# Expert products of 64 stationary columns in place of two of 32, in a mixture-of-experts encoder block

## The chip, the cores and the metric

The kernel runs on one core of a Trainium2 chip. The metric is the device time of one execution in microseconds, as the median of three runs. A profile comes from one further execution, which has a time of its own.

## The reference, cut to what matters

The block is one layer: a mixer (a gated DeltaNet and a short convolution, side by side), then a mixture of experts, each behind a modulated RMSNorm with a gated residual, and a last RMSNorm. There are 256 positions of width 1024, and all data are float32. The change touches only the experts:

```python
logits = hf @ router_w + router_b            # 256 tokens, 32 experts
top_val, top_idx = lax.top_k(logits, 4)      # each token goes to 4 experts
gates = softmax(top_val)
...
gu = x_blk @ w1[e] + b1[e]                   # w1[e]: 1024 x 2048
gate, up = split(gu, 2)
act = min(gate, 7) * sigmoid(1.702 * gate) * (clip(up, -7, 7) + 1)
yb = act @ w2[e] + b2[e]                     # w2[e]: 1024 x 1024
...
y = segment_sum(yb * gate_of_token)          # back to the 256 tokens
```

## The kernel before

**Stages.** The mixer and the routing come first. The experts begin at about 427 us of the profiled execution, and it is their stage that the change touches. The weights of all 32 experts (w1 8 MB and w2 4 MB each) are read once from HBM, in float32, through a ring of buffers (`wst`) that SP's queue fills in program order.

**Slots.** Experts are taken four at a time, in eight quads `q`. A quad has 256 slots, in eight groups of 32. `GROUPS` (line 31) says how many groups each of the four experts has: (2, 2, 2, 2) in the first quad, (3, 1, 2, 2) in the other seven. A quad is two pairs `p = 2*q + pa`, each with two experts `m` and four groups of slots, 128 slots in all. So the owners of the four groups of a pair are 0, 0, 1, 1 in both pairs of quad 0 and in the second pair of every quad, and 0, 0, 0, 1 in the first pair of quads 1 to 7 (p = 2, 4, ..., 14).

**Products.** The tokens of the slots are the stationary operand and the weights are the moving one. `w1_pair` (line 1409) goes over eight blocks `k` of 128 rows of w1 and four stretches `c` of 512 columns of it; for each (k, c) it issues four products of 32 stationary columns, one for each group of slots, at `tile_position=(0, 32 * j)`. Each of them writes its own 32 partitions of the accumulator `pss[c]`. `Second.block` (line 1459) does the same with the activations `aT` and w2, for eight blocks `f` and two halves `h`, in place of four stretches. `w2_cols` (line 1479) does it for the last pair, in three parts of the columns. Below, the four products of one (k, c) or (f, h) are called a set. All these products are issued by the helper `mm` (line 1336), so they all carry line 1337 in the profile; they are told apart by their operands: `acc<-wst,XT` for w1 and `acc<-wst,aT` for w2.

**Order.** The order of TensorE's work is that of the program (`held = [pin]`). In the loop over pairs (line 1674) the first product of pair p comes first, then the second product of pair p - 1 by blocks, and between the blocks hang the small steps: transposes of the activations (`to_ff`), the gather of the next quad's tokens (`gather_part`), and the combine step (`combine`), whose products are 128 columns wide. Each pair begins with four bias products (`w1_bias`, line 120), so the rows of line 120 mark the pairs in time.

**Two other places** are used below for comparison. `three_pass` (lines 312 to 314) issues the mixer's projections, most of them with 128 stationary columns; its call from `ba_mm` (line 447) has 32 and no tile position. Lines 943 and 944 issue two products of 64 stationary columns at `tile_position=(0, 64 * h)`.

Of the kernel before, what the change touches and what calls it, by code (L numbers as in the profile page):

```python
# [21 lines left out]
KT = D // 128  # L22
# [8 lines left out]
GROUPS = ((2, 2, 2, 2), (3, 1, 2, 2))  # L31
# [22 lines left out]
def encoder_block(ctx, tc, x, c, ada_w, ada_b, norm1_w, w_in, conv_qkv_w, a_log, dt_bias, onorm_w,  # L54
# [59 lines left out]
    def acc():  # L114
        return pm.tile([128, 512], FT, name="acc", tag=next(accs), bufs=3)

    def w1_bias(pa, bsel, b1c, pss, parts=(0, 1, 2, 3), first=False, pinned=False):
        for c in parts:
            b = 32 * c
            i = PE.matmul(pss[c], bsel[b:b + 32, pa * 128:(pa + 1) * 128], b1c[b:b + 32], start=first, stop=not first,  # L120
                          tile_position=(b, 0), skip_group_check=True)
            if pinned:
                tc.keep_in_program_order(i)
# [10 lines left out]
    with ExitStack() as mix:  # L134
# [119 lines left out]
        class Job:  # L254
            def __init__(self, load, cut, mm, post=None, lo="v"):
                self.load, self.cut, self.mm, self.post, self.lo, self.parts = load, cut, mm, post, lo, None
# [95 lines left out]
        for j in range(4):  # L352
# [12 lines left out]
            w = ep.tile([128, KT, 256], FT, name="raw", tag="raw", bufs=6) \  # L365
# [13 lines left out]
            for kk in range(2):  # L379
                k = 2 * j + kk  # L380
# [118 lines left out]
        for d in range(2):  # L499
            m = masks[:, d]  # L500
# [488 lines left out]
        def load_rows(srcs, hold=lambda i: i):  # L989
            _, halves = slot()  # L990
            for h, src in zip(halves, srcs):
                hold(nc.sync.dma_start(h, src))
            return halves
# [14 lines left out]
        def w1_load(p, k, regs):  # L1008
            if p < 2 or p == 2 * NQ - 1 and k >= KT - 2:
                return pre.pop((p, k), None) or w1_rows(p, k, regs)  # L1010
            if k % 2 == 0:
                c = 256 * (k // 2)
                held_w[0] = [load_unit(w1_src(p, m, regs)[:, c:c + 256]) for m in range(2)]
            return [quarters(h[k % 2]) for h in held_w[0]]
# [157 lines left out]
        def flat(x):  # L1172
            for it in x:
                if isinstance(it, (list, tuple)):
                    yield from flat(it)
                else:
                    yield it
        tail, n = list(flat(late_items)), 0
# [143 lines left out]
    for p, k, m, ts in ((0, KT - 1, 0, [spare("g"), spare("g"), spare("u"), spare("th")]),  # L1322
                        (0, KT - 1, 1, [spare("ysb"), spare("ysb"), spare("pg"), spare("pgT")]),
                        (1, 4, 0, [spare("aT", 1024), spare("aT", 1024)]), (1, 4, 1, [e4, fw])):
        o, qs = 0, []
        c = 256 * (k // 2) + k % 2
        for t in ts:
            n = t.shape[1]
# [7 lines left out]
    def mm(*a, **kw):  # L1336
        return held[0](PE.matmul(*a, **kw))  # L1337
# [17 lines left out]
    def gather_part(P, xq, ks):  # L1355
        p = misc()
        for kk, k in enumerate(ks):
            o = p[:, kk * QS:(kk + 1) * QS]
            n = 0
            for t in range(2):  # L1360
                for hx in (h2h, h2l):
                    mm(o, hx[:, t, 256 * (k // 2) + k % 2:256 * (k // 2) + k % 2 + 255:2], P[:, t],
                                  start=n == 0, stop=n == 3, skip_group_check=True)
                    n += 1
        for kk, k in enumerate(ks):
            o = p[:, kk * QS:(kk + 1) * QS]
            if k % 2:
                V.tensor_scalar(xq[:, k], o, facp[:, k:k + 1], facp[:, 8 + k:9 + k], op0=OP.mult, op1=OP.add)  # L1368
            else:
                A.activation(xq[:, k], o, AF.Identity, scale=facp[:, k:k + 1], bias=facp[:, 8 + k:9 + k])  # L1370
# [15 lines left out]
        A.copy(gt, p.rearrange("p (a t n) -> p a t n", a=2, t=2))  # L1386
        return gt

    def owners(q):
        return [m for m, g in enumerate(GROUPS[min(q, 1)]) for _ in range(g)]  # L1390

    def swiglu(n, g_ps, u_ps):
        g = work.tile([128, 512], FT, name="g", tag="g", bufs=2)
# [14 lines left out]

    def w1_pair(p, xq, bsel, pss, regs, mids):
        q, pa = divmod(p, 2)  # L1410
        own = owners(q)[4 * pa:4 * pa + 4]
        if p:
            w1_bias(pa, bsel, b1c, pss, first=True, pinned=True)
        for k in range(KT):
            w = w1_load(p, k, regs)
            for c in (0, 2, 1, 3):
                for j in range(4):
                    mm(pss[c][j * 32:(j + 1) * 32], xq[:, k, (4 * pa + j) * 32:(4 * pa + j + 1) * 32],
                                  w[own[j] % 2][c], start=False, stop=k == KT - 1,
                                  tile_position=(0, 32 * j), skip_group_check=True)  # L1420
            if p == 0 and k < KT - 2:
                gather_part(P0, xq, (k + 2,))
            for f in mids.get(k, ()):
                f()
        return [swiglu(128, pss[half], pss[2 + half]) for half in range(2)]
# [18 lines left out]
    def w2_rows(p, m, regs):  # L1444
        return moe_w2[0, 2 * p + m:2 * p + m + 1] if p < 2 else moe_w2[0, ds(regs[2 * (p % 2) + m], 1)]
# [7 lines left out]
    class Second:  # L1453
        def __init__(self, p, aT, gt, regs):
            self.p, self.aT, self.gt, self.regs = p, aT, gt[:, p % 2], regs
            self.own = owners(p // 2)[4 * (p % 2):4 * (p % 2) + 4]
            self.ys = [acc() for _ in range(2)]

        def block(self, c):
            if self.p < 2 or self.p == 2 * NQ - 2:  # L1460
                w = load_rows([w2_rows(self.p, m, self.regs)[:, 512 * (c // 2):512 * (c // 2) + 512]
                               .rearrange("e (p s r) n -> s p (e r n)", s=2, r=2)[c % 2] for m in range(2)])
            else:
                if c % 2 == 0:
                    self.w = [load_unit(w2_rows(self.p, m, self.regs)[:, 256 * c:256 * c + 512]) for m in range(2)]
                w = [h[c % 2] for h in self.w]
            w = [h.rearrange("p (i n) -> p i n", i=2) for h in w]
            for i in range(2):
                f = 2 * c + i
                for h in range(2):  # L1470
                    for j in range(4):
                        mm(self.ys[h][j * 32:(j + 1) * 32], self.aT[:, f, j * 32:(j + 1) * 32],
                           w[self.own[j] % 2][:, i, 512 * h:512 * h + 512], start=f == 0, stop=f == KT - 1,
                           tile_position=(0, 32 * j), skip_group_check=True)

        def end(self):
            return [lambda h=h, y=scaled(self.ys[h], 512 * h, 512): combine([self.gt], [y], 512 * h, 512) for h in range(2)]

    def w2_cols(p, parts, aT, gt, regs):
        q, pa = divmod(p, 2)  # L1480
        own = owners(q)[4 * pa:4 * pa + 4]
        c0, n = parts[0][0], sum(n for _, n in parts)
        ys = [acc() for _ in parts]
        nc_ = 2 if n > 256 else 4
        for c1 in range(0, 4, nc_):
            w = []
            for m in range(2):
                src = w2_rows(p, m, regs)[:, 256 * c1:256 * c1 + 256 * nc_, c0:c0 + n]
                if n > 256:
                    w.append(load_unit(src, 2 * n, True))  # L1490
                else:
                    _, halves = slot()
                    for h in range(2):
                        nc.sync.dma_start(halves[h][:, 0:4 * n].rearrange("p (i n) -> p i n", n=n),
                                          src[:, 512 * h:512 * h + 512].rearrange("e (p i) n -> p (e i) n", i=4))
                    w.append([halves[c // 2][:, 2 * n * (c % 2):2 * n * (c % 2) + 2 * n] for c in range(4)])
            w = [[h[:, 0:2 * n].rearrange("p (i n) -> p i n", i=2) for h in hs] for hs in w]
            for c in range(nc_):
                for i in range(2):
                    f = 2 * (c1 + c) + i  # L1500
                    for y, (o, no) in zip(ys, parts):
                        for j in range(4):
                            mm(y[j * 32:(j + 1) * 32, 0:no], aT[:, f, j * 32:(j + 1) * 32],
                                          w[own[j] % 2][c][:, i, o - c0:o - c0 + no], start=f == 0, stop=f == KT - 1,
                                          tile_position=(0, 32 * j), skip_group_check=True)
        return [lambda o=o, no=no, y=scaled(y, o, no): combine([gt[:, pa]], [y], o, no) for y, (o, no) in zip(ys, parts)]

    gtf_box = []
# [100 lines left out]
    xq = xq_tile()  # L1609
# [64 lines left out]
    for p in range(NP):  # L1674
        q, pa = divmod(p, 2)
# [32 lines left out]
        if 0 < p < NP - 1:  # L1708
# [4 lines left out]
            if pa and q + 1 < NQ:  # L1713
                xq = xq_tile()
# [28 lines left out]
    with tc.If(n_over > 0):  # L1743
        ov = work.tile([128, KT, 128], FT, name="over", tag="aT", bufs=2).rearrange("p b n -> p (b n)")
        V.tensor_tensor(rks[:, 0], rks[:, 0], capr[:, None, :].to_broadcast([128, 2, NE]), op=OP.subtract)
        with tc.For_i(0, NE, 1) as cp:
# [6 lines left out]
            with tc.For_i(0, nb, 1) as b:  # L1753
# [7 lines left out]
                p = misc()  # L1761
                for k in range(KT):
                    n = 0
# [8 lines left out]
                p = misc()  # L1772
# [4 lines left out]
                for half in range(2):  # L1777
                    pss = [acc() for _ in range(2)]
                    for gu in range(2):
                        bs = slice(32 * (2 * gu + half), 32 * (2 * gu + half) + 32)  # L1780
                        PE.matmul(pss[gu][0:32], ohe[bs].to_broadcast([NE, 32]), b1c[bs],
                                  start=True, stop=False, tile_position=(bs.start, 0), skip_group_check=True)
                    for k in range(KT):
                        wo = wp_box[0].tile([128, 2, 512], FT, name="wst", tag="u5")
                        for gu in range(2):
                            c0 = gu * FF + half * 512
                            nc.sync.dma_start(wo[:, gu], moe_w1[0, ds(e, 1), k * 128:(k + 1) * 128, c0:c0 + 512]
                                              .rearrange("e p n -> p (e n)"))
                        for gu in range(2):
                            PE.matmul(pss[gu][0:32], xo[:, k], wo[:, gu], start=False, stop=k == KT - 1,  # L1790
                                      skip_group_check=True)
                    act_t(32, swiglu(32, *pss), aTo[:, half * 4:half * 4 + 4, :])
                for half in range(2):
                    y = acc()
                    for f in range(KT):
# [5 lines left out]
                                  skip_group_check=True)  # L1801
# [49 lines left out]
```

## Time and profile before

| | us |
|---|---|
| median of three runs | 1365.51 (1365.5 to 1365.85) |
| time of the profiled execution | 1366.79 |
| its span, from the first to the last instruction | 1364.9 |
| TensorE busy in the span | 1267.2 (93%) |
| mean granted TensorE clock, as a share of full | 0.982 |

The span is shorter than the time of its execution by 1.9 us. Busy time counts the time in which at least one product runs, with modelled ends, so a busy TensorE can still be one with most of its array at rest. PE is TensorE's products and PEld its weight loads; DVE is VectorE, ACT is ScalarE, POOL is GpSimd and SP is SyncE, and a q behind one of them is its queue.

### The profile page before, as it was taken

Reading aid. Unit: us, or ns where it says so; the run is one execution under the profiler, and the core shown is the slowest. Engines: PE = TensorE matmul, PEld = TensorE weight load, DVE = VectorE, ACT = ScalarE, POOL = GpSimd, SP = SyncE. Lnnn points to the kernel's source line nnn. Section 1 sums busy time; section 2 is a strip of 40 time slices with the busy share of each in tenths; the row PEclk is TensorE's granted clock in tenths of the full one; section 3 lists DMA queues with packets and bytes.
Section 4 is the critical chain, followed back from the end, with each engine's and each line's share of the span. In section 5 each row is a group of like instructions: output and inputs, shape, how many; then the busy total and the mean of one; then the engine's idle time right before and its main releaser. Section 6 shows DMA issues by size and latency. Waiting matters only on the chain. (4 is left out here: it accounts for less than half of the span.)

```text
span 1364.9 us, 24037 instructions
## 1 busy us (share of the span) xinstructions
PE 1267.2 (93%) x10284; PEld 663.1 (49%) x10285; DVE 514.7 (38%) x1019; ACT 281.9 (21%) x546; POOL 150.3 (11%) x127
## 2 busy tenths in 40 slices
PE   6999997999999999999998989989989899998986
PEld 4898886999997333233333223322322232232222
DVE  3377879975774231232222112121211212221113
ACT  3455552554543010000001000000100000010001
POOL 4555685000000000000000000000000000000000
PEclk9999998999999999999999999989999898999998
DMA  9978978226798999999999999999999999999994
GB/s 337 303 248 270 327 238 255 73 93 222 243 381 307 422 427 369 419 426 427 425 426 423 429 424 426 423 428 426 425 424 427 425 426 424 425 428 424 422 409 161
DMA packets 114753, 492.65 MB, mean 361 GB/s; under 512 B 8910, under 2 KB 64591, under 8 KB 82769
## 3 DMA queue, kind: packets, MB, share of 16 engines
q1 hardware_dynamic: 110400, 485.94, 89.3%
q10 hardware_dynamic: 4241, 5.12, 1.1%
q8 instruction: 82, 1.34, 0.4%
q14 instruction: 30, 0.25, 0.1%
HBM read 486.82 MB, written 4.21 MB: 360 GB/s over the span
## 5 line engine op out<-in xcount | busy, mean ns | idle before, releaser
L1337 PE MATMUL acc<-wst,XT 128*32 128x512 f32 x4088 | 472.5, 596 | 15.0 <-DMA wst<-in_moe_w_dram 14.9
L1337 PE MATMUL acc<-wst,aT 128*32 128x512 f32 (+1 forms) x2112 | 259.3, 604 | 40.7 <-DMA wst<-in_moe_w_dram 40.6
L1337 PEld LDWEIGHTS acc<-wst,XT 128*32 128x32 f32 x4088 | 133.8, 110 | 328.6 <-issue 293.9
L1337 PEld LDWEIGHTS acc<-wst,aT 128*32 128x32 f32 x2112 | 69.8, 113 | 199.5 <-issue 131.9
L312 PE MATMUL mm<-hh,wh 128*128 128x256 f32 (+1 forms) x520 | 150.4, 289 | 1.3 <-DVE cacc L560 1.3
L314 PE MATMUL mm<-hh,wl 128*128 128x256 f32 (+1 forms) x520 | 149.5, 288 | 1.8 <-POOL wl L264 1.3
L313 PE MATMUL mm<-hh,wh 128*128 128x256 f32 (+1 forms) x520 | 149.5, 288 | 0.0
L263 ACT CAST wh<-raw 128x1024 fp32r<-128x1024 f32 (+1 forms) x89 | 91.9, 1039 | 93.4 <-PE mm L313 59.5
L312 PEld LDWEIGHTS mm<-hh,wh 128*128 128x128 f32 (+1 forms) x520 | 99.7, 192 | 10.9 <-issue 6.7
L88 POOL TENSOR_TENSOR rs<-ss,half_m 128x2 f32<-128x2 f32 x3 | 2.1, 716 | 932.2 <-DVE ss L1812 874.8
L314 PEld LDWEIGHTS mm<-hh,wl 128*128 128x128 f32 (+1 forms) x520 | 99.7, 192 | 5.8 <-issue 2.5
L1396 DVE TENSOR_SCALAR g<-acc 128x512 f32<-128x512 f32 x32 | 22.0, 688 | 209.8 <-PE acc L1337 209.8
L313 PEld LDWEIGHTS mm<-hh,wh 128*128 128x128 f32 (+1 forms) x520 | 99.7, 192 | 0.9 <-issue 0.8
L264 POOL TENSOR_TENSOR wl<-raw,wh 128x1024 fp32r<-128x1024 f32 x36 | 87.6, 2442 | 72.5 <-ACT wh L263 65.6
L1442 DVE TENSOR_TENSOR x<-x,misc 128x512 f32<-128x512 f32 (+1 forms) x66 | 44.2, 671 | 121.9 <-PE misc L1337 121.9
L1397 ACT ACTIVATE th<-g 128x512 f32<-128x512 f32 x32 | 20.2, 630 | 325.8 <-DVE g L1396 274.8
L1449 DVE TENSOR_TENSOR ysb<-acc,gtf 128x512 f32<-128x512 f32 (+1 forms) x33 | 22.3, 676 | 147.9 <-PE acc L1337 147.7
L264 DVE TENSOR_TENSOR wl<-raw,wh 128x1024 fp32r<-128x1024 f32 (+1 forms) x53 | 63.7, 1209 | 29.0 <-ACT wh L263 28.6
L1337 PE MATMUL misc<-ysb,pgT 128*128 128x512 f32 (+1 forms) x132 | 63.9, 606 | 0.3 <-ACT aT L1433 0.2
L1368 DVE TENSOR_SCALAR XT<-misc,fac 128x256 f32<-128x256 f32 x32 | 17.4, 543 | 118.7 <-ACT XT L1370 97.4
L560 DVE SCALAR_TENSOR_TENSOR cacc<-mm,col,cacc 128x254 f32<-128x254 f32 (+1 forms) x96 | 46.1, 480 | 9.0 <-ACT cacc L557 6.9
L1370 ACT ACTIVATE XT<-misc,fac 128x256 f32<-128x256 f32 x32 | 18.1, 566 | 141.8 <-PE misc L1337 141.8
(387 smaller groups left out, 1368.2 us busy)
## 6 DMA issues: line engine op xcount, KB each, us to landing
wst<-in_moe_w_dram SPq DMA_DIRECT2D x123, 2048.0 KB, 29.5
wst<-in_moe_w_dram SPq DMA_DIRECT2D x126, 1024.0 KB, 20.9
raw<-in_w_in_dram SPq DMA_DIRECT2D x36, 1024.0 KB, 7.3
raw<-in_ada_w_dram SPq DMA_DIRECT2D x24, 1024.0 KB, 8.9
wst<-in_moe_w_dram SPq DMA_DIRECT2D x8, 768.0 KB, 17.0
raw<-in_w_out_sc_dram SPq DMA_DIRECT2D x4, 1024.0 KB, 7.3
raw<-in_w_up_a_dram SPq DMA_DIRECT2D x4, 1024.0 KB, 5.2
raw<-in_w_o_dram SPq DMA_DIRECT2D x4, 1024.0 KB, 9.3
```

Source lines behind the costliest of these rows:

```text
L263: a = A.copy(wh, src)
L264: b = (V if job.lo == "v" else G).tensor_tensor(wl, src, wh.bitcast(FT), op=OP.subtract)
L312: PE.matmul(ps, wh[:, k, :], ah[:, k, :], start=k == 0, stop=False, skip_group_check=True)
L313: PE.matmul(ps, wh[:, k, :], al[:, k, :], start=False, stop=False, skip_group_check=True)
L314: PE.matmul(ps, wl[:, k, :], ah[:, k, :], start=False, stop=k == KT - 1, skip_group_check=True)
L560: V.scalar_tensor_tensor(a[:, o0:o1], p[:, s0:s1], cw(j), a[:, o0:o1], op0=OP.mult, op1=OP.add)
L1337: return held[0](PE.matmul(*a, **kw))
L1370: A.activation(xq[:, k], o, AF.Identity, scale=facp[:, k:k + 1], bias=facp[:, 8 + k:9 + k])
L1396: V.tensor_scalar(g[:n], g_ps[:n], 7.0, None, op0=OP.min)
L1397: A.activation(th[:n], g[:n], AF.Tanh, scale=0.851)
L1442: V.tensor_tensor(xv, xv, p[:, 0:n], op=OP.add)
L1449: V.tensor_tensor(y, ps[:, 0:n], gtf_box[0][:, c0:c0 + n], op=OP.mult)
```

## The change

A new generator, `tiles_of(p)`, takes the place of `owners(q)`. It joins two neighbouring groups of 32 slots of one expert into one of 64, where the first of them stands at slot 0 or 64. The three places that issue expert products then issue one product for each of the joined stretches. With owners 0, 0, 1, 1 a set becomes two products of 64 columns. With owners 0, 0, 0, 1 it becomes one of 64, one of 32 (slots 64 to 95) and one of 32 (slots 96 to 127, the other expert). Nothing else is changed: loads, buffers, bias products and the order of the steps stay.

```diff
-    def owners(q):
-        return [m for m, g in enumerate(GROUPS[min(q, 1)]) for _ in range(g)]
+    def tiles_of(p):
+        q, pa = divmod(p, 2)
+        own = [m % 2 for m, g in enumerate(GROUPS[min(q, 1)]) for _ in range(g)][4 * pa:4 * pa + 4]
+        off = 0
+        while off < 4:
+            n = 2 if off % 2 == 0 and own[off] == own[off + 1] else 1
+            yield slice(32 * off, 32 * off + 32 * n), own[off]
+            off += n
...
     def w1_pair(p, xq, bsel, pss, regs, mids):
-        own = owners(q)[4 * pa:4 * pa + 4]
+        own = list(tiles_of(p))
...
             for c in (0, 2, 1, 3):
-                for j in range(4):
-                    mm(pss[c][j * 32:(j + 1) * 32], xq[:, k, (4 * pa + j) * 32:(4 * pa + j + 1) * 32],
-                                  w[own[j] % 2][c], start=False, stop=k == KT - 1,
-                                  tile_position=(0, 32 * j), skip_group_check=True)
+                for r, m in own:
+                    mm(pss[c][r], xq[:, k, 128 * pa + r.start:128 * pa + r.stop], w[m][c], start=False, stop=k == KT - 1,
+                       tile_position=(0, r.start), skip_group_check=True)
...
     class Second:
...
-                    for j in range(4):
-                        mm(self.ys[h][j * 32:(j + 1) * 32], self.aT[:, f, j * 32:(j + 1) * 32],
-                           w[self.own[j] % 2][:, i, 512 * h:512 * h + 512], start=f == 0, stop=f == KT - 1,
-                           tile_position=(0, 32 * j), skip_group_check=True)
+                    for r, m in self.own:
+                        mm(self.ys[h][r], self.aT[:, f, r], w[m][:, i, 512 * h:512 * h + 512], start=f == 0,
+                           stop=f == KT - 1, tile_position=(0, r.start), skip_group_check=True)
...
     def w2_cols(p, parts, aT, gt, regs):
...
-                        for j in range(4):
-                            mm(y[j * 32:(j + 1) * 32, 0:no], aT[:, f, j * 32:(j + 1) * 32],
-                                          w[own[j] % 2][c][:, i, o - c0:o - c0 + no], start=f == 0, stop=f == KT - 1,
-                                          tile_position=(0, 32 * j), skip_group_check=True)
+                        for r, m in own:
+                            mm(y[r, 0:no], aT[:, f, r], w[m][c][:, i, o - c0:o - c0 + no], start=f == 0, stop=f == KT - 1,
+                               tile_position=(0, r.start), skip_group_check=True)
```

## Rows read from the trace of the kernel before

**Rows 1.** The page's slices of the span: busy tenths, DMA share, GB/s.
```profile
PE   6999997999999999999998989989989899998986
...
DMA  9978978226798999999999999999999999999994
GB/s 337 303 248 270 327 238 255 73 93 222 243 381 307 422 427 369 419 426 427 425 426 423 429 424 426 423 428 426 425 424 427 425 426 424 425 428 424 422 409 161
```

**Rows 2.** Groups by line and shape: count, then busy us, mean ns of one.
```profile
L1337 PE MATMUL acc<-wst,XT 128*32 128x512 f32 x4088 | 472.5, 596 | 15.0 <-DMA wst<-in_moe_w_dram 14.9
L1337 PE MATMUL acc<-wst,aT 128*32 128x512 f32 x1984 | 254.2, 618 | 40.7 <-DMA wst<-in_moe_w_dram 40.6
...
L1337 PE MATMUL misc<-ysb,pgT 128*128 128x512 f32 x124 | 61.7, 619 | 0.3 <-ACT aT L1433 0.2
```

**Rows 3.** Stretches: length, busy us of each engine, PEclk, DMA share, GB/s.
```profile
500.00:600.00 100.00, 98.08 (x802) 33.68 (x798) 23.81 (x54) 9.70 (x17) 0.00 (x0) 1.00 0.97 406
600.00:700.00 100.00, 98.62 (x813) 32.97 (x808) 25.22 (x50) 7.00 (x12) 0.00 (x0) 1.00 1.01 426
979.40:1099.90 120.50, 108.24 (x853) 34.64 (x852) 24.65 (x52) 7.57 (x13) 0.00 (x0) 0.97 1.01 426
...
521.40:1365.00 843.60, 771.88 (x6167) 253.22 (x6166) 183.29 (x377) 57.22 (x103) 0.74 (x1) 0.98 0.98 412
```

**Rows 4.** Waits of PE from 521 us to the end: us, times, longest.
```profile
PE acc L1337 <- DMA wst<-in_moe_w_dram: 55.5, 28, 5.3
```

**Rows 5.** Timeline of PE, bias products: start of pairs 2 to 5, 10, 12.
```profile
521.41 1.14 PE L120 MATMUL acc<-b1c,bsel 32*128 32x512 f32 x8
...
572.88 1.14 PE L120 MATMUL acc<-b1c,bsel 32*128 32x512 f32 x8
...
630.70 1.14 PE L120 MATMUL acc<-b1c,bsel 32*128 32x512 f32 x8
...
678.51 1.14 PE L120 MATMUL acc<-b1c,bsel 32*128 32x512 f32 x8
...
979.45 1.14 PE L120 MATMUL acc<-b1c,bsel 32*128 32x512 f32 x8
...
1099.93 1.14 PE L120 MATMUL acc<-b1c,bsel 32*128 32x512 f32 x8
```

**Rows 6.** Timeline of weight loads about pair 9's start: start, us, what, idle before.
```profile
917.62 0.14 PEld L1337 LDWEIGHTS acc<-wst,XT 128*32 128x32 f32 x4 [0.76 <-issue]
...
918.05 0.15 PEld L1337 LDWEIGHTS acc<-wst,XT 128*32 128x32 f32 x6 [0.28 <-DMA wst<-in_moe_w_dram]
...
918.50 0.12 PEld L1337 LDWEIGHTS acc<-wst,XT 128*32 128x32 f32 x4 [0.31 <-issue]
...
920.65 0.12 PEld L1337 LDWEIGHTS acc<-wst,XT 128*32 128x32 f32 x2 [0.31 <-issue]
921.61 0.30 PEld L1337 LDWEIGHTS misc<-ysb,pgT 128*128 128x128 f32 x2 [0.84 <-issue]
922.14 0.19 PEld L1337 LDWEIGHTS misc<-ysb,pgT 128*128 128x128 f32 x1 [0.24 <-issue]
922.57 0.19 PEld L1337 LDWEIGHTS misc<-ysb,pgT 128*128 128x128 f32 x1 [0.24 <-issue]
923.52 0.16 PEld L1337 LDWEIGHTS acc<-wst,XT 128*32 128x32 f32 x8 [0.76 <-issue]
923.98 0.13 PEld L1337 LDWEIGHTS acc<-wst,XT 128*32 128x32 f32 x4 [0.30 <-issue]
```

**Rows 7.** Timeline at 56.7 us: 32 columns without a tile position, behind 128.
```profile
56.73 0.28 PE L339 MATMUL dd<-hh,wl 128*128 128x256 f32 x1
56.73 0.11 PEld L312 LDWEIGHTS mm<-hh,wh 128*32 128x32 f32 x1
```

**Rows 8.** Timeline at 313 us: lines 943 and 944, loads and products.
```profile
313.29 0.20 PEld L943 LDWEIGHTS pt<-fac,ident 128*64 128x64 f32 x4
...
313.29 0.29 PE L943 MATMUL pt<-fac,ident 128*64 128x8 f32 x4
```

More of the change, by code (lines that the diff above doesn't have):

```diff
@@ L1455, in __init__ @@
             self.p, self.aT, self.gt, self.regs = p, aT, gt[:, p % 2], regs
-            self.own = owners(p // 2)[4 * (p % 2):4 * (p % 2) + 4]
+            self.own = list(tiles_of(p))
             self.ys = [acc() for _ in range(2)]
@@ L1480, in w2_cols @@
         q, pa = divmod(p, 2)
-        own = owners(q)[4 * pa:4 * pa + 4]
+        own = list(tiles_of(p))
         c0, n = parts[0][0], sum(n for _, n in parts)
```

## Prediction

> **What bounds the kernel now.** I read the slices of the page first [rows 1]. From the fourteenth slice on, which is the experts' stage, the DMA engines are busy nine tenths or more nearly throughout and move about 425 GB/s; TensorE shows eight to nine tenths as well. So two candidates stand close together, and the question is how much room the second has under the first. The groups by line [rows 2] say what TensorE does there: w1_pair has 16 x 8 x 4 x 4 = 2048 products, and 4088 are recorded, so a float32 product goes through the array in two passes. The mean pass lasts 596 ns, and 4088 of them are busy for only 472.5 us: they overlap about fivefold, by the modelled ends.
>
> The timeline of weight loads gives the true pace [rows 6]. At 918.50 four loads start together, and the same row, idle time included, returns every 0.43 us until 920.65 (918.93, 919.36 and so on are left out). So four tiles of 32 columns run side by side, each pass takes 0.43 us, and a set of four products (eight passes) takes 0.86 us. The 128-column products of the combine step have the same pace: 922.14 to 922.57 is 0.43 us. A pass thus costs its 512 moving columns, whatever its width.
>
> The room: pair 4 runs from 630.70 to 678.51, 47.8 us, and pair 3, which also gathers tokens, from 572.88 to 630.70, 57.8 us [rows 5]. From 500 to 700 us TensorE is busy for 98 to 99% at the full clock (the first two rows of [rows 3]). A quad costs it about 105.6 us. Quad 5 took 120.5 us from 979.45 to 1099.93 [rows 5] with DMA share at its top, and there TensorE was busy for 108.2 us, modelled ends included [rows 3]. So weights bound the kernel, and TensorE has about 15 us in 120 to spare. Counted over the rest of the program from pair 2 on, at 521.41 [rows 5]: TensorE waits for weights for 55.5 us in 28 waits [rows 4]; and the granted clock is 0.98 over 843.6 us [rows 3], which is about 17 us lost at the lower of its two levels (1.2 in place of 2.4 GHz), after such waits.
>
> **The change part by part.** There are 16 x 48 sets and 8 more in w2_cols: 776. In 440 of them (owners 0, 0, 1, 1) four products of 32 become two of 64; in 336 (seven pairs, 32 sets of w1 and 16 of w2) four become one of 64 and two of 32.
>
> *The 440 even sets.* Two products of 64 side by side stream the same 512 columns, so a set stays at two passes of 0.43 us if the halves run together. Lines 943 and 944 show that they can: four loads of 64 columns take 0.20 us together, the four passes 0.29 us [rows 8]. Were the second half to wait, each set would cost 0.86 us more, 378 us in all; those rows speak against it. I take 0. The 880 products that go save no time, for their passes lay beside others.
>
> *The 336 mixed sets.* Here tiles of 64 and of 32 columns follow each other, twice a set. The trace has no such neighbours, so I bound the price. Below: the three run side by side on their own columns, as the four do now, and the set stays at 0.86 us. Above: one width waits until the other is through. What a change of tile costs is seen at both ends of a combine step [rows 6]. The last row of loads of 32 is at 920.65; one more pass follows without a load, so the array is free of streaming at 920.65 + 2 x 0.43 = 921.51, and the next load, of 128 columns, is at 921.61: 0.10 us later. Its own time isn't hidden either: the second pass starts at 922.14, 0.53 us on, not 0.43. The way back is the same: 922.57 + 0.86 = 923.43, load at 923.52, second pass at 923.98, 0.46 us on. So a change of tile costs 0.10 us of rest, and the bare load: 0.10 us for 128 columns, 0.03 for 32, and by the middle 0.05 for 64. Between passes of one tile form loads cost nothing.
>
> Is it the width or the tile form that makes the array run empty? The form [rows 7]: a load of 32 columns *without* a tile position starts at 56.73, together with the 128-column pass before it, and is hidden. Both times the columns of the new load are in use by the running product, so a conflict of columns is not the reason. Line 943's tiles of 64 are a form of their own and line 1337's of 32 another; the nearest changes are those of [rows 6], and they wait. I therefore take the upper bound: a mixed set is 64 (two passes, 0.86) + change to 32 (0.13) + the two of 32 side by side (0.86) + change to 64 (0.15) = 1.99 us, 1.13 us more than now. 336 x 1.13 = 380 us.
>
> The Trainium skill speaks to this. Its page "TensorEngine Tiling (Array Packing)", section "Key Properties", says that changing the tiling mode, not just the tile, drains TensorE, and it lists 128x64 and 128x32 as separate modes. The trace agrees where it has a change of mode (0.10 us of rest [rows 6]) and has none from 64 to 32; by the rule the sum is that of the upper bound, 1668 us below. [...]
>
> *The sum.* TensorE's need from pair 2 on grows by 380 us. It first eats the room: the waits for weights, 55.5 us plus some 0.165 us for each of the 28 (a pass is modelled 0.59 us long and streams for 0.43), 60 us; and the clock, 17 us, for without the waits I expect the full clock, as there. So 1364.9 + 380 - 60 - 17 = 1668 us of span. By quads it comes to nearly the same: 48 x 1.13 = 54 us more in quad 1, which has no room yet (521.41 to 630.70 is 109.3 us [rows 5]); 105.6 + 54 = 160 in place of 120 us in quads 2 to 6, 200 us; and some 45 in the last: 299 us. The profiled execution has 1.9 us outside its span and lies 1.3 us above the median; so 1668 us for the median.
>
> *Small parts.* The bias products, gathers, transposes and combine steps keep their count and form; the changes of tile around them stay, with a load of 64 in place of 32 (0.02 us each, some hundred times, 2 us, left out of the sum). What VectorE and ScalarE do with a pair (24 to 25 us and 7 to 10 us busy in 100 [rows 3]) lies under TensorE's longer pairs. SP's queue fills the ring further ahead and then waits for TensorE to free buffers; nobody waits for it.
>
> **The rivals.**
>
> *Side by side (no change).* The 64 and the 32s run at once on their own strips. For it: tiles of 32 already run independently; at 917.62 the first expert's two tiles start and load their next weights while the other two wait until 918.05 for a transfer, and each keeps its own phase [rows 6]. Against it: the change of form [rows 6, 7]. It decides if a mixed set's three products start within 0.05 us of each other. Then TensorE needs what it needed, weights bound the kernel: 1365.5 us.
>
> *One behind the other, without rest.* The widths exclude each other, but the next load is hidden: 0.86 us a mixed set, 288 us, less 77: 1576 us. Against it: both changes shown rest [rows 6].
>
> *A change at every pass.* The two passes of the 64 alternate with those of the 32s, four changes a set: 1.13 + 0.28 = 1.41 us, 474 less 77: 1762 us. Against it: the loads for the second pass follow at once behind those of the first (x8 at 923.52 in [rows 6]).
>
> *Faster.* Only the tail behind the last weights could gain, and its sets keep their passes; I see no row for it.
>
> **How the numbers follow.** One behind the other with rest 0.76; without rest 0.06; a change at every pass 0.04; side by side 0.12; faster 0.02. The prediction is 1668 us. The range from 1560 to 1770 us holds the first three cases with what is uncertain in them (the room of 77 us, the rest per change) and leaves out 0.14 and a little of the first. A measurement tells apart 0.2%, 2.7 us: faster 0.02, same 0.12, slower 0.86.
>
> **What would show it.** Right: pairs 2, 4, ... have rows of 64 columns that alternate with rows of 32, a set every 2 us; the even pairs' sets return every 0.86 us; a quad takes about 160 us from bias row to bias row; GB/s falls from 425 to some 315 in the experts' stage; PE's waits for weights vanish and the clock is at 1.00 there. Wrong: mixed sets every 0.86 us with DMA still at 425 GB/s (side by side), or sets of two 64s that take 1.7 us (the halves exclude each other), or a clock that falls in the mixed sets, where part of the array rests: that would add up to as much again as the time at the lower level.

## The result, and the profile after

The changed kernel takes 1643.34 us (median of five runs, 1642.41 to 1644.02), the kernel before 1365.5 us: 1.203 times as long, with a 95% interval of 1.202 to 1.205. The prediction was 1668 us, with a range of 1560 to 1770 us.

The slices of the page of the kernel after (busy tenths, granted clock, DMA share, GB/s) and the stretch from pair 2 to the end (length, busy us of each engine, PEclk, DMA share, GB/s) answer to [rows 1] and [rows 3]:

```profile
PE   7999989999999999999999999999999999999997
...
PEclk9999999999999999999999999999999999999999
DMA  9789762479898589658966895698669857966890
GB/s 339 251 282 312 252 210 84 179 230 352 331 423 376 205 321 426 280 221 363 427 249 275 370 428 226 239 427 363 257 274 427 354 236 302 427 278 252 361 361 27
```
```profile
521.40:1641.50 1120.10, 1106.24 (x4057) 283.20 (x4056) 184.63 (x377) 57.20 (x103) 0.74 (x1) 1.00 0.76 310
```

The two candidates have changed places. TensorE is busy in all but the edges of the experts' stage, at the full clock. The DMA engines have gaps: in each quad the rate falls from some 427 GB/s to between 205 and 257, by the slices, and comes back; its mean is 310 GB/s. It is low in the mixed pairs (243 GB/s in pair 10, 392 in pair 11), where SP's queue waits for TensorE to free buffers (from pair 2 on, at line 981, 692.9 us in all; before it was 153.3 us).

The groups by line and shape (count, then busy us, mean ns of one) answer to [rows 2]:

```profile
L1337 PE MATMUL acc<-wst,XT 128*64 128x512 f32 x1596 | 497.3, 602 | 0.0
L1337 PE MATMUL acc<-wst,aT 128*64 128x512 f32 x768 | 241.7, 601 | 0.0
L1337 PE MATMUL acc<-wst,XT 128*32 128x512 f32 x896 | 235.7, 605 | 0.0
...
L1337 PE MATMUL acc<-wst,aT 128*32 128x512 f32 x448 | 117.8, 605 | 0.0
```

Fewer products, each as long as before, are busy for longer: the 4088 passes with `XT` filled 472.5 us before, the 2492 of now fill 733 us. The columns behind the second bar, which held waits for weights of 14.9 and 40.6 us, are at 0.0.

The timeline of weight loads in an even pair and in a mixed one (start, us, what, idle before) answers to [rows 6]:

```profile
1078.18 0.20 PEld L1337 LDWEIGHTS acc<-wst,XT 128*64 128x64 f32 x4 [0.76 <-issue]
1078.66 0.14 PEld L1337 LDWEIGHTS acc<-wst,XT 128*64 128x64 f32 x2 [0.29 <-issue]
1079.09 0.14 PEld L1337 LDWEIGHTS acc<-wst,XT 128*64 128x64 f32 x2 [0.29 <-issue]
1079.52 0.14 PEld L1337 LDWEIGHTS acc<-wst,XT 128*64 128x64 f32 x2 [0.29 <-issue]
```
```profile
1007.40 0.14 PEld L1337 LDWEIGHTS acc<-wst,XT 128*32 128x32 f32 x4 [0.81 <-issue]
1008.38 0.19 PEld L1337 LDWEIGHTS acc<-wst,XT 128*64 128x64 f32 x2 [0.84 <-issue]
1009.38 0.14 PEld L1337 LDWEIGHTS acc<-wst,XT 128*32 128x32 f32 x4 [0.81 <-issue]
1010.36 0.19 PEld L1337 LDWEIGHTS acc<-wst,XT 128*64 128x64 f32 x2 [0.84 <-issue]
1011.37 0.14 PEld L1337 LDWEIGHTS acc<-wst,XT 128*32 128x32 f32 x4 [0.81 <-issue]
```

In the even pair (the first fence) two loads of 64 come together every 0.43 us: one pass of both halves, side by side, so a set takes 0.86 us as it did with four tiles of 32. In the mixed pair the 64 loads at 1008.38 and the 32s only at 1009.38, when the 64's two passes are through, although the 32s' own columns (64 to 127) have been at rest all that time. The next 64 loads at 1010.36. A set takes 1.98 us, and the idle time before each load is 0.81 to 0.84 us in place of 0.29: no load is hidden under a pass of the other form.

Bias products mark pairs 10, 11 and 12 (start, us, what) as in [rows 5]:

```profile
993.49 1.14 PE L120 MATMUL acc<-b1c,bsel 32*128 32x512 f32 x8
...
1077.11 1.14 PE L120 MATMUL acc<-b1c,bsel 32*128 32x512 f32 x8
...
1148.85 1.14 PE L120 MATMUL acc<-b1c,bsel 32*128 32x512 f32 x8
```

Pair 10 takes 83.6 us and pair 11 71.7 us, together 155.4 us, where quad 5 took 120.5 us.

### The profile page after: what moved, and what is told of

The parts are those of the page before. It is cut to its first block, busy times and chain, and to the rows that moved or that the text cites. A ratio compares the mean times of both kernels' runs of the same rounds, so it can differ in the third digit from the quotient of the medians.

```text
span 1641.5 us, 19173 instructions
## 1 busy us (share of the span) xinstructions
PE 1602.6 (98%) x7852; PEld 695.9 (42%) x7853; DVE 516.6 (31%) x1019; ACT 282.0 (17%) x546; POOL 151.2 (9%) x127
## 5 line engine op out<-in xcount | busy, mean ns | idle before, releaser
L1337 PE MATMUL acc<-wst,XT 128*64 128x512 f32 (+1 forms) x2492 | 703.3, 603 | 0.0
L1337 PEld LDWEIGHTS acc<-wst,XT 128*64 128x64 f32 (+1 forms) x2492 | 153.6, 126 | 528.0 <-issue 520.5
L1337 PE MATMUL acc<-wst,aT 128*64 128x512 f32 (+2 forms) x1280 | 351.8, 591 | 0.0
L1337 PEld LDWEIGHTS acc<-wst,aT 128*64 128x64 f32 (+1 forms) x1280 | 80.1, 126 | 248.0 <-issue 241.0
```

## The experiments

The theory: 64 columns and 32 columns are two forms of the array, and one waits until the other is through, with 0.10 us of rest and a bare load at each change. Its rivals: products of 64 are dear by themselves, or a mixed set is dear for another reason than its changes. And a question of size: the time came out 25 us under the prediction, so is the price of a set or the room under the weights off?

**One half of the change at a time.** In the kernel after, joined tiles only where the owners are 0, 0, 1, 1; then only where they are 0, 0, 0, 1:

```diff
-            n = 2 if off % 2 == 0 and own[off] == own[off + 1] else 1
+            n = 2 if sum(own) == 2 and off % 2 == 0 and own[off] == own[off + 1] else 1
```

> Joined tiles of 64 only in the nine pairs with owners 0, 0, 1, 1 (440 sets); the seven mixed pairs keep four products of 32. Theory (only a neighbourhood of 64 and 32 costs): 1365.5 us, within 3 us, sets of two 64s every 0.86 us. Rival (products of 64 columns are dearer by themselves, the halves exclude each other): 440 x 0.86 = 378 us more, less the room of some 100 us, about 1640 us.

Measured: 1362.93 us, 0.998 of the kernel before on its chip (1365.74 us), interval 0.997 to 0.999. The rival of 1640 us is ruled out. The theory had no change, and there is a small gain. As the weights bound this kernel, a cost smaller than the room would not show in its time; the next run closes that gap.

The other half has `sum(own) == 1` in the same place.

> Joined tiles only in the seven mixed pairs (336 sets of one 64 and two 32); the even pairs keep four products of 32. Theory: the whole loss, 1643 us within 5 us. Rival (the even pairs share in it): between 1366 and 1635 us.

Measured: 1642.96 us, 1.2026 times the kernel before (1.2008 to 1.2044). The 336 mixed sets carry the whole loss. TensorE bounds this kernel and the kernel after alike; they differ only in the 440 even sets, four products of 32 here and two of 64 there, and their times lie 0.4 us apart (those of the kernel before, in the same two measurements, 0.6 us). So the even sets cost nothing that these runs could show.

**Fewer changes, as many passes.** In the mixed pairs all 64s of a block go first, then all 32s:

```diff
-            for c in (0, 2, 1, 3):
+            for wide in (True, False):
+              for c in (0, 2, 1, 3):
                 for r, m in own:
+                    if (r.stop - r.start > 32) != wide:
+                        continue
...
-                for h in range(2):
+                for h, wide in ((0, True), (1, True), (0, False), (1, False)):
                     for r, m in self.own:
+                        if (r.stop - r.start > 32) != wide:
+                            continue
```

> The kernel after, with the products of a mixed pair sorted by tile form: all four 64s of a block k, then its eight 32s; in the second product the 64s of both halves, then the 32s. Changes of form fall from 8 to 2 in a block of w1 and from 4 to 2 in a block of w2; the passes stay. Theory (a change costs 0.10 us of rest and the bare load): 6 x 0.135 = 0.8 us saved in each of 7 x 8 blocks of w1 and 2 x 0.135 = 0.27 us in each of 7 x 8 blocks of w2, 60 us: about 1583 us. The rest of the loss, 0.86 us a set, stays, since 64s and 32s still run one behind the other. Rival (what costs is the set, not the change): 1643 us. Rival (without a change in every set the forms overlap): below 1450 us.

Measured: 1583.35 us, 1.159 times before (1.1575 to 1.1613), 60 us less than after. The theory had 1583 us; the rivals, 1643 us and below 1450 us, are ruled out. Its loads in one block of a w1 product (start, us, what, idle before):

```profile
1132.88 0.19 PEld L1337 LDWEIGHTS acc<-wst,XT 128*64 128x64 f32 x2 [0.76 <-issue]
1133.36 0.14 PEld L1337 LDWEIGHTS acc<-wst,XT 128*64 128x64 f32 x1 [0.29 <-issue]
...
1135.51 0.14 PEld L1337 LDWEIGHTS acc<-wst,XT 128*64 128x64 f32 x1 [0.29 <-issue]
1136.46 0.14 PEld L1337 LDWEIGHTS acc<-wst,XT 128*32 128x32 f32 x4 [0.81 <-issue]
1136.91 0.12 PEld L1337 LDWEIGHTS acc<-wst,XT 128*32 128x32 f32 x2 [0.31 <-issue]
```

Among the 64s loads are hidden (idle 0.29 us, a pass every 0.43 us). The eight passes of four 64s take from 1132.88 to 1136.46, 3.58 us, and only then come the 32s. The loss that remains, 218 us, is that of one form behind the other and of the two changes left in a block, less the room that is derived below.

**As many products, one form.** A mixed set as three products of 64:

```diff
+        if sum(own) == 1:
+            yield from ((slice(0, 64), 0), (slice(64, 128), 0), (slice(64, 128), 1))
+            return
```

(and `start` and `stop` set at the first and the last of the two that share slots 64 to 127).

> The kernel after, with a mixed set as three products of 64 columns: slots 0 to 63 with the first expert, slots 64 to 127 with the first and once more with the second expert, summed in one place, so that the last 64 slots of these pairs get other sums than the reference's. As many products a set as after, all of one form. Theory (the change of form costs the rest and the overlap, and a set lasts as long as its busiest columns): four passes on slots 64 to 127, 1.71 us a set, with the passes of slots 0 to 63 beside them and no rest; 0.857 us more than before, 288 us, less the room of some 95 us: 1558 us. Rival (three products in a set cost what they cost after): 1643 us. Rival (three 64s exclude each other): six passes, 2.57 us a set, 1.71 us more: 1845 us.

Measured: 1560.31 us, 1.1426 times before (1.1409 to 1.1444), where the theory had 1558 us. Its loads in a mixed pair:

```profile
690.81 0.19 PEld L1337 LDWEIGHTS acc<-wst,XT 128*64 128x64 f32 x3 [0.29 <-issue]
691.24 0.14 PEld L1337 LDWEIGHTS acc<-wst,XT 128*64 128x64 f32 x1 [0.23 <-issue]
691.66 0.14 PEld L1337 LDWEIGHTS acc<-wst,XT 128*64 128x64 f32 x1 [0.29 <-issue]
692.09 0.14 PEld L1337 LDWEIGHTS acc<-wst,XT 128*64 128x64 f32 x1 [0.29 <-issue]
692.52 0.20 PEld L1337 LDWEIGHTS acc<-wst,XT 128*64 128x64 f32 x3 [0.29 <-issue]
```

A set takes 1.71 us (690.81 to 692.52): the four passes of slots 64 to 127, with the two of slots 0 to 63 beside them. With as many products as after but no change of form there is overlap and no rest. So neither the count of products nor their width is what costs.

**The room under the weights, from two sides.** First more work without a change of form, in the kernel before:

```diff
-            for c in (0, 2, 1, 3):
+            for n, c in enumerate(((0, 0, 0) if p > 1 else ()) + (0, 2, 1, 3)):
...
-                                  w[own[j] % 2][c], start=False, stop=k == KT - 1,
+                                  w[own[j] % 2][c], start=False, stop=k == KT - 1 and (p < 2 or n > 2),
```

> The kernel before, with three more sets of four 32s in every block of w1 from pair 2 on (the first set of the block issued four times in all, so its sums are other than the reference's): 14 x 24 = 336 sets of 0.857 us, 288 us of TensorE work with no change of form. Theory (TensorE's room under the weights is some 100 us, as 1365.5 + 379 - 1643 gives it): 1365.5 + 288 - 102 = 1552 us. Rival (the room is 77 us as the prediction had it, and a mixed set costs less than 1.13 us): 1576 us.

Measured: 1559.14 us (1557.16 to 1561.14). 288 us were added and 193 us came out: the room is 95 us.

Then fewer weights, in the kernel before:

```diff
-            if k % 2 == 0:
+            if k % 4 == 0 or p == 15 and k == 4:
                 c = 256 * (k // 2)
                 held_w[0] = [load_unit(w1_src(p, m, regs)[:, c:c + 256]) for m in range(2)]
```

> The kernel before, with half of the w1 loads left out from pair 2 on (each loaded unit is used for two neighbouring pairs of blocks, so the products are other than the reference's): a third less to load for a pair, and TensorE has the same work. Theory (room of some 100 us): 1365.5 - 102 = 1263 us, with no waits of TensorE for weights. Rival (room of 77 us): 1288 us. If the weights did not bound the kernel: 1365 us.

Measured: 1273.47 us, 0.932 of before (0.931 to 0.934): the room is 92 us. Both stand nearer to the theory's 102 us than to 77 us, and both fall short of it. Pairs 10 to 12 of this kernel, which no longer waits for weights:

```profile
938.86 1.14 PE L120 MATMUL acc<-b1c,bsel 32*128 32x512 f32 x8
986.67 1.14 PE L120 MATMUL acc<-b1c,bsel 32*128 32x512 f32 x8
1040.90 1.14 PE L120 MATMUL acc<-b1c,bsel 32*128 32x512 f32 x8
```

TensorE's need is 47.8 us for pair 10 and 54.2 us for pair 11, and so a mixed set's price can be had from pairs that wait for no weights in either kernel: (83.6 - 47.8) / 32 = 1.12 us in pair 10, (71.7 - 54.2) / 16 = 1.09 us in pair 11.

**The small gain once more.**

> The same kernel as the run with joined tiles in the even pairs only, once more and against more runs of the kernel before. It had come out 2.8 us faster, where the theory had no change. If that gain is real it comes again, 1362 to 1364 us, with an upper end of the interval under 1; if not, 1365.5 us.

Measured: 1363.64 us against 1366.12 us, 0.9984 (0.9975 to 0.9993). It is real and smaller than the 0.2% that a single measurement can tell. In the first of the two profiles TensorE's last wait for weights that is over 1 us ends at 1323.85 us in place of 1325.87 us. Why the weights end earlier was not settled. Of the kernels here that load all weights and do the whole work, this one is the fastest.

## Why the prediction was right, and where it was off

*The mechanism.* "One width waits until the other is through" held, with its price: a mixed set takes 1.98 us in the timeline, the prediction had 1.99; the change costs 0.10 us of rest and the bare load, which the sorted kernel's 60 us show by themselves. What carried it was the comparison of two rows of the kernel before: a load of 32 columns with a tile position waits [rows 6], one without is hidden [rows 7], both on columns in use. It pointed to the form, and the form it was. By themselves the two rows left a doubt, for they differ in type as well: the operands of [rows 7] are cast to fp32r, and a product there is one pass. The kernel before has the same pair in float32, in the transposes of line 1340 and the expert products behind them:

```profile
462.85 0.27 PE L1340 MATMUL misc<-ident,gat 128*128 128x128 f32 x1
462.86 0.10 PEld L1340 LDWEIGHTS misc<-ident,rk 128*32 128x32 f32 x1
...
463.07 0.27 PE L1340 MATMUL misc<-ident,gat 128*128 128x128 f32 x1
...
463.27 0.16 PEld L1337 LDWEIGHTS acc<-wst,XT 128*32 128x32 f32 x8 [0.17 <-issue]
```

The transposes follow each other every 0.11 us. Behind a pass of 128 columns, 32 without a tile position load at once (462.86); 32 with one load only at 463.27, 0.20 us behind the pass of 463.07, which is the 0.11 us of its streaming and 0.09 us of rest. So it is the form, and neither the width nor the type.

The rule of the Trainium skill's page "TensorEngine Tiling (Array Packing)", section "Key Properties" (a change of tiling mode drains TensorE), agrees with the runs: 64 and 32 columns behave as two modes, and a set that changes between them takes 1.98 us.

The rival of side by side does not hold across forms: after, the 32s wait for the 64 on columns that it doesn't use. Among tiles of one form it holds, here for 64 too (a pass of both halves every 0.43 us).

*The even sets.* Priced at 0, from [rows 8]; the run with these alone came out 0.2% under, not over. The ground was weaker than the outcome: the passes in [rows 8] have 8 moving columns, so those rows show the halves loading side by side and not 512 columns streaming so. The 0.86 us a set after shows that.

*The sum.* It was 25 us too high, in two terms. The first: 336 x 1.13 = 380 us was 373 us, 7 x (35.8 + 17.5). Where a combine step or a gather stands between two sets, its own changes were there before as well, and I had charged each set two full changes. The second, the larger: the room was put at 77 us, 60 of waits and 17 of clock, and measured 92 to 95 us. Both errors went the same way. With 373 and 95 the sum is 1365.5 + 373 - 95 = 1643.5 us, with 92 it is 1646.5 us. The expectations' 102 us was the price's 379 less the measured difference, and so carried the same error of 6 or 7 us.

Where the missing 15 to 18 us of room were: I had taken PE's waits [rows 4], which count only the time in which no product runs. From pair 2 on the same products kept PE busy for 771.9 us before [rows 3] and for 734.6 us in the run with fewer weights, which waits for none (stretch, length, then PE's busy us first):

```profile
521.40:1274.00 752.60, 734.57 (x6174) 244.24 (x6172) 183.60 (x378) 57.24 (x103) 0.74 (x1) 0.99 0.78 311
```

So 37 us of the busy time before did no more work, and with the 55.5 us of waits they make 93 us, the room as measured. The sum had 17 us of the 37 for the clock (15 us by the means of the whole span: 0.982 of 1364.9 us before and 0.994 of 1641.5 us after lose 24.6 and 9.8 us) and 5 us for modelled ends. Some 15 us more were not in it. A tile that waits while another runs counts as busy: at 918.05 in [rows 6] the second expert's two tiles start 0.43 us behind the first's. That the 15 us are made of such times is worked out from these rows, not tried in a run.

*By quads* the same gap has another face: 105.6 us for a quad took pair 3 as typical, and with 54.2 us for an odd pair a quad needs 102.0 us. Pair 3 carries the second bias (`second_bias`), which comes once. By the rows of line 120 in both kernels quad 1 grew by 51.8 us, quads 2 to 6 by 190.5 and the last by 34.0; the prediction had 54, 200 and "some 45", for which it gave no row.

*The signs.* All came as listed: sets of 2 us in the mixed pairs and 0.86 us in the even ones, 155 us a quad (160 predicted), 310 GB/s (315), no waits of PE for weights, and the clock at 1.00. The clock that falls where part of the array rests did not come.

## What to carry to other kernels

Before joining or splitting tiles, look at whether neighbours in the stream keep one form: four products of 32 columns were as fast as two of 64, and a 64 with two 32s took 2.3 times as long, though no column was shared. Where mixed forms can't be avoided, sort by form, and count the passes of each form on its busiest columns, add them up, and add 0.10 us and a bare load for each switch. To size the room under another bound, don't read it from the waits of an engine that runs several tiles: take the work away from the bound, or add some that has a known price, and see.

## What the runs showed of the hardware

The array takes 512 columns of float32 in 0.43 us for a pass of 32, 64 or 128 stationary columns, and tiles of one form keep their own phases: in the run with three 64s one half makes four passes while the other makes two. Tiles of 64 and 32 exclude each other even on separate columns; with rest at the change this was foreseen at 0.76. The rest was taken over from changes between 32 and 128 columns (0.10 us); take four passes of 0.43 us and two bare loads (0.03 and 0.05 us) from a mixed set's 1.98 us, and 0.09 us is left for each change between 64 and 32 too. What makes the rest was not tried. A small gain of 0.16 to 0.2% from fewer, wider products in a stage that weights bound was not foreseen and has no cause shown.
